# Three pairs of gate columns by Strassen, and the S5 branch in five steps per block

## The chip, the cores and the metric

The kernel runs on one core of a Trainium2 chip. The metric is the time of one execution on the device, in microseconds. The core has a matrix engine (TensorE, PE in the profile), whose weight loads are shown apart (PEld), three engines for elementwise work (VectorE or DVE, ScalarE or ACT, GpSimd or POOL) and a queue that issues transfers (SyncE or SP). Each engine executes its own instructions strictly in the order in which they were written, and waits at an instruction until what it reads has been written and what it overwrites has been read.

## The reference

One layer of a decoder trunk for 1024 tokens of width 1024, all in float32, cut to what matters here:

```
h = rms_norm(x, g_pre)
proj = h @ w_in
s5_x, s5_g, lru_x, lru_g, gate_s, gate_l = split(proj)   # 512, 512, 1280, 1280, 1024, 1024 columns
y_s = s5_ssm(s5_x, ...)                  # complex diagonal recurrence over the tokens
y_s = glu(gelu(y_s) @ w_glu) * silu(s5_g);  z_s = y_s @ w_bs
y_l = rg_lru(conv(lru_x), ...);             z_l = (y_l * silu(lru_g)) @ w_bl
merged = sigmoid(gate_s) * z_s + sigmoid(gate_l) * z_l
x = x + rms_norm(merged @ w_out, g_post)
x = x + (p @ w_ple) * sigmoid(x @ w_ple_gate)
```

The result must keep float32 accuracy. Each matrix product is therefore three products of rounded operands: high x high, high x low and low x high part.

## The kernel before, in words

Tensors lie transposed: 128 channels on the partitions, tokens along the row. h is four operands (B11, B21 for the first 512 tokens, input rows 0 to 511 and 512 to 1023; B12, B22 for the other 512), each in a high and a low part. `w_in` is 44 columns of 128 outputs. A column takes 8 row blocks x 2 token halves x 3 = 48 products of 128x512 (function `rows`), accumulated in PSUM, and `light` passes it through a sigmoid on ScalarE and stores it. Columns 36 to 43 are gate_l, 28 to 35 gate_s, 4 and 5 part of s5_g.

The class `Weights` streams weights: SP loads chunks of eight 128x128 blocks into four raw buffers; for every four blocks ("quad") ScalarE writes the high part into one of six ring buffers (L222) and VectorE the low part (L234), four quads ahead of TensorE. For some weights the low part is made by ScalarE and an accumulating transfer that GpSimd issues (L226).

The order is written by hand for TensorE, VectorE, ScalarE and GpSimd; only SP's order comes from the scheduler. Small work runs beside the columns: generators in the list `bg` are advanced one step by each `tick()`, and `rows` ticks after every 12 products, four times per column. A step only says where instructions stand in each engine's order; an engine may be ahead of TensorE or late.

S5 is such a generator. First the parameters (`prep`), on VectorE and then on GpSimd; three idle ticks; the ladders (`s5_ladders`: two tables of powers by doubling, 4 and 3 steps of four VectorE operations); "powers" (`powers_zoh`, seven VectorE operations, L669 to L675); `turn`: pwT, four transposes of it on TensorE (L691), evicted by ScalarE and sent through HBM (pt_d) into every block's wn. Then eight blocks (`s5_main`), a block seven ticks apart from the next:

1. VectorE multiplies wn (L913, L915);
2. the block before is finished: output products py (L983, L984), GELU on ScalarE; the next block's loads are issued;
3. products pkt on TensorE, four copies kt on ScalarE, an addition, and eight transfers that spread kt into the matrix toep, which py reads;
4. products pin (L939);
5. ScalarE copies pin to pq, VectorE rotates it by the tables (ta, tb, q); GpSimd makes the next block's output weights ca (L902 to L904, its middle operation waits for the toep transfers, since it writes the buffer of kt);
6. the scan (L960) and the rotation back; 7. the last four operations q (L971, L972), which py reads.

The next block's table (`s5_table`) is spread over these steps. After S5 its memory goes to the LRU branch. The later stages (`w_bl`, `w_out`) already use Strassen's scheme with seven half-size products.

## Time and profile before

| | |
|---|---|
| median of 3 runs | 928.81 us (928.27 to 928.93) |
| the profiled execution: time, span | 928.25 us, 926.5 us |
| gate columns and S5 (77.8 to 300.5 us) | 18 columns of 48 products and 8 blocks |
| DMA over the span | 134.21 MB, mean 145 GB/s |

A row of the timeline gives start, duration, engine, line, operation, output and inputs, shapes and count; in brackets how long the engine sat idle before it and what ended that. A row of a window gives, for each engine, busy time and number of instructions, then the granted clock, the busy share of the DMA engines and GB/s. A matmul's shown duration is longer than its distance to the next, since matmuls overlap; what a product costs is read from start to start. A 128x128 product on unrounded float32 counts as two instructions.

### The profile page before, as it was taken

The numbers are of one execution on the slowest core, as the hardware profiler recorded it, in microseconds if no ns is written. First come the engines' busy times: TensorE is split into PE (matmuls) and PEld (weight loads), VectorE is DVE, ScalarE is ACT, GpSimd is POOL, SyncE is SP. The second block draws the span as 40 slices with busy tenths as digits, with TensorE's granted clock in tenths as the row PEclk, the third lists the DMA queues.
The fourth block names the chain that finished last, engine by engine and source line by source line (L and its number), as shares of the span: only waits on it lengthen the run. The fifth ranks groups of instructions, "written<-read, shape, count | busy, mean of one in ns | idle before, by whom it ended". The sixth has DMA issues, their size and how long they took to land.

```text
span 926.5 us, 11716 instructions
## 1 busy us (share of the span) xinstructions
PE 919.0 (99%) x4228; PEld 760.3 (82%) x4228; DVE 624.6 (67%) x977; ACT 469.1 (51%) x714; POOL 150.6 (16%) x159
## 2 busy tenths in 40 slices
PE   9999999999999999999999999999999999999997
PEld 7888888888888888888888888888888887887886
DVE  6885566666664347766666767687862798886863
ACT  6643233444443356666666668544534355558531
POOL 1218112212220000000000000022322126422100
PEclk9999999999999999999999999999999999999999
DMA  9745445564533201111111116811479975499951
GB/s 358 277 126 160 126 142 166 172 171 133 173 97 113 74 29 52 52 46 51 52 52 52 47 34 216 291 56 55 141 255 244 247 193 206 119 245 233 301 184 56
DMA packets 70442, 134.21 MB, mean 145 GB/s; under 512 B 18416, under 2 KB 32880, under 8 KB 70384
## 3 DMA queue, kind: packets, MB, share of 16 engines
q1 hardware_dynamic: 64768, 122.72, 41.7%
q0 software_dynamic: 5472, 10.49, 6.3%
q8 instruction: 33, 0.54, 0.2%
q10 hardware_dynamic: 144, 0.26, 0.1%
q14 instruction: 25, 0.20, 0.1%
HBM read 95.30 MB, written 27.53 MB: 133 GB/s over the span
## 4 chain that ended last, share of the span: by engine, by line
PE 89%; issue 6%; DMA 2%; DVE 1%; POOL 1%; ACT 0%; POOLq 0%; SPq 0%
PE ps_L L319 16%; PE ps_L L317 8%; PE ps_rx L319 8%; PE ps_rg L319 8%; PE ps_rg L317 4%; PE ps_rx L317 4%; PE ps_F L319 3%; PE ps_u L319 3%; PE bZ L319 3%; PE ps_pg L319 2%; PE bW L319 2%; PE pg L319 2%; PE bX L319 2%; PE ps_ple L319 2%; PE ps_ea L319 2%
## 5 line engine op out<-in xcount | busy, mean ns | idle before, releaser
L319 PE MATMUL ps_L<-hB,wq 128*128 128x512 f32 x640 | 197.4, 390 | 0.0
L319 PEld LDWEIGHTS ps_L<-hB,wq 128*128 128x128 f32 x640 | 120.3, 188 | 24.3
L317 PE MATMUL ps_L<-hB,wq 128*128 128x512 f32 x320 | 127.1, 397 | 0.0
L222 ACT ACTIVATE wq<-wraw 128x512 fp32r<-128x512 f32 (+1 forms) x188 | 112.5, 613 | 24.1 <-issue 9.2
L234 DVE TENSOR_TENSOR wq<-wraw,wq 128x512 fp32r<-128x512 f32 (+1 forms) x152 | 105.0, 706 | 3.1 <-ACT wq L222 3.1
L319 PE MATMUL ps_rg<-hB,wq 128*128 128x512 f32 x320 | 98.5, 389 | 0.0
L319 PE MATMUL ps_rx<-hB,wq 128*128 128x512 f32 x320 | 98.5, 389 | 0.0
L319 PE MATMUL ps_pg<-x1hl,wq 128*128 128x512 f32 x240 | 74.9, 392 | 0.3 <-DVE x1hl L1374 0.2
L317 PEld LDWEIGHTS ps_L<-hB,wq 128*128 128x128 f32 x320 | 60.2, 188 | 13.3 <-issue 1.7
L319 PEld LDWEIGHTS ps_rg<-hB,wq 128*128 128x128 f32 x320 | 60.1, 188 | 12.5
L319 PEld LDWEIGHTS ps_rx<-hB,wq 128*128 128x128 f32 x320 | 60.1, 188 | 12.4
L194 POOL TENSOR_TENSOR wS<-wraw 128x512 f32<-128x512 f32 x8 | 12.4, 1549 | 354.8 <-DMA wraw<-w_blocks 343.3
L1078 DVE SCALAR_TENSOR_TENSOR c<-ps_rx,cp_t,c 128x1023 f32<-128x1023 f32 (+2 forms) x30 | 38.5, 1282 | 46.2 <-ACT c L1076 45.5
L317 PE MATMUL ps_rx<-hB,wq 128*128 128x512 f32 x160 | 62.3, 389 | 0.0
L317 PE MATMUL ps_rg<-hB,wq 128*128 128x512 f32 x160 | 62.3, 389 | 0.0
L319 PEld LDWEIGHTS ps_pg<-x1hl,wq 128*128 128x128 f32 x240 | 44.8, 188 | 11.5 <-DVE x1hl L1374 1.7
L1015 ACT ACTIVATE sg<-ps_L 128x1024 f32<-128x1024 f32 x20 | 20.5, 1027 | 59.7 <-issue 52.5
L226 POOL DMA_DIRECT2D wq<-wraw x36 | 31.8, 883 | 100.1 <-ACT wq L225 65.6
L317 PE MATMUL ps_pg<-x1hl,wq 128*128 128x512 f32 x120 | 47.0, 391 | 0.0
L319 PE MATMUL ps_u<-hB,wq 128*128 128x512 f32 x128 | 39.8, 392 | 0.4 <-DVE hB L736 0.4
L319 PE MATMUL ps_F<-ys,wq 128*128 128x512 f32 x128 | 39.4, 389 | 0.0
L1086 ACT ACT_TABLE_LOAD x9 | 11.5, 1283 | 51.2 <-DVE yr L1115 51.2
(360 smaller groups left out, 1927.0 us busy)
## 6 DMA issues: line engine op xcount, KB each, us to landing
wraw<-w_blocks SPq DMA_DIRECT2D x95, 512.0 KB
wq<-wraw POOLq DMA_DIRECT2D x36, 256.0 KB, 6.0
xt<-x_t SPq DMA_DIRECT2D x8, 512.0 KB
ple_d<-ple_sb SPq DMA_DIRECT2D x8, 512.0 KB
wn<-sbt SPq DMA_DIRECT2D x8, 512.0 KB
sgl_d<-sg SPq DMA_DIRECT2D x8, 512.0 KB
wn<-pt_d SPq DMA_DIRECT2D x16, 256.0 KB
sgs_d<-sg SPq DMA_DIRECT2D x8, 512.0 KB
```

Of the source, the lines that this page charges most:

```text
L194: G.tensor_tensor(s[name], s[a], s[b], op)
L222: nc.scalar.activation(hi, src, AF.Copy)
L226: nc.gpsimd.dma_start(lo.bitcast(F32), src, accum_op=ALU.add)
L234: self.nc.vector.tensor_tensor(lo, src, hi.bitcast(F32), ALU.subtract)
L317: T.matmul(ps, wh, xh, start=start, stop=False, skip_group_check=more)
L319: T.matmul(ps, a, b, start=False, stop=stop and a is (wh if xl_last else wl), skip_group_check=more)
L1015: S.activation(t, ps, AF.Sigmoid)
L1078: V.scalar_tensor_tensor(c[:, d:], ps[:, :NT - d], w_[3 - d], c[:, d:], ALU.mult, ALU.add)
L1086: S.activation(sq, ps, AF.Sigmoid)
```

## The change

Columns 30 to 35 of `w_in` are made in three pairs (30 and 31, 32 and 33, 34 and 35). With a pair's weights cut into A11, A12 (column m, input rows 0 to 511 and 512 to 1023) and A21, A22 (column m + 1), the pair is

```
S1 = A21 + A22   S2 = S1 - A11   S3 = A11 - A21   S4 = A12 - S2
T1 = B12 - B11   T2 = B22 - T1   T3 = T2 - B11    T4 = B21 - T2
u = A11*B11      z = u + S2*T2   w = S1*T1
column m:     first tokens u + A12*B21      other tokens z + w + S4*B22
column m + 1: first tokens z + S3*T3 + A22*T4      other tokens z + w + S3*T3
```

Seven products of four blocks (12 products of 128x512 each) stand for eight. The two of the first line's column m (bank lX) come first for all three pairs, then the other five pair by pair (banks lZ, two halves z and w). For these columns VectorE makes the sums S that GpSimd makes for `w_bl`, and the low parts of the plain quads and of A22 go the way by transfer.

The T need h in float32, so each of its eight row blocks is written to HBM (`h_d`) when it is made, and quarters of it come back into pages (`h_load`). T1 and T2 are subtracted on VectorE beside the last two S5 blocks (`t_early`), T3 and T4 after S5, where all four are also cut into high and low parts (`t_build`), with four pages and two buffers in the memory that S5 gave back.

S5's steps 1 and 2, and 3 and 4, are merged, so that a block takes five ticks. Columns 4 and 5 come first now, and S5 runs beside these two and the ten columns 36 to 43, 28 and 29. The ladders and the first table are a generator of their own (`s5_first`) ahead of `s5_all` in the list, the idle ticks are gone, and powers follow the end of `prep` by one tick and `turn` by two.

```
@@ -60,8 +61,16 @@
     plain(col("w_in", 2, lo) + col("w_in", 0, hi))
     plain(col("w_in", 1, hi) + col("w_in", 2, hi))
     plain(col("w_in", 3, range(ND)))
-    for m in (*range(36, 44), *range(28, 36), 4, 5):
+    for m in (4, 5, *range(36, 44), *range(28, PAIRS[0])):
         plain(col("w_in", m, range(ND)))
+    for m in PAIRS:
+        c = chunk(col("w_in", m, range(ND)))
+        light.add(c)
+        cut(c)
+    for m in PAIRS:
+        c0, c1 = (chunk(col("w_in", m + i, range(ND))) for i in range(2))
+        light.add(c0)
+        quads.extend((part, c0, c1, 4) for part in ("O2", "S1", "S3", "S4", "A22"))

     def gated(m, head):
         c = chunk(col("w_in", m, range(ND)))
...
@@ -191,7 +201,7 @@
                     s[name] = self.tmp.tile([P, HT], F32, tag=name, name=f"w{name}_{i}")
                 else:
                     s[name] = s[into]
-                G.tensor_tensor(s[name], s[a], s[b], op)
+                (self.nc.vector if light else G).tensor_tensor(s[name], s[a], s[b], op)

             if q[0] == "plain":
                 _, c, o, n = q
...
@@ -205,7 +215,7 @@
                 add("S1", "A21", "A22", ALU.add)
                 add("S2", "S1", "A11", ALU.subtract)
             if q[0] in ("S4", "O4"):
-                add("S4", "A12", "S2", ALU.subtract, "S2")
+                add("S4", "A12", "S2", ALU.subtract, "A12" if light else "S2")
             if q[0] == "S3":
                 add("S3", "A11", "A21", ALU.subtract, "A21")
             self.ready.append((s[q[0].replace("O", "S")], 4))
...
@@ -221,7 +231,8 @@
             lo = t[:, 1].rearrange("p b m -> p (b m)")[:, :n * P]
             nc.scalar.activation(hi, src, AF.Copy)
             q = QUADS[i]
-            if q[0] == "plain" and BLOCKS[q[1][0]][0] in self.BY_DMA and i < len(QUADS) - 2 * ND:
+            if q[0] in ("plain", "A22") and (q[1] in LIGHT or BLOCKS[q[1][0]][0] in self.BY_DMA
+                                             and i < len(QUADS) - 2 * ND):
                 nc.scalar.activation(lo, src, AF.Copy, scale=-1.0)
                 nc.gpsimd.dma_start(lo.bitcast(F32), src, accum_op=ALU.add)
             else:
...
@@ -734,6 +746,7 @@
         for h in range(2):
             hi, lo = hplain(k, h)
             (G if h and k else V).tensor_tensor(lo, xt(k, HALF[h]), hi.bitcast(F32), ALU.subtract)
+        nc.sync.dma_start(h_d[k], xt(k))

     def h_pages(names):
         for n, i0 in names:
...
@@ -917,9 +930,10 @@
         G.tensor_tensor(
             dd, ident[:16, :16].unsqueeze(1).to_broadcast([16, 4, 16]),
             d_skip[:, 4 * hb:4 * hb + 4].unsqueeze(2).to_broadcast([16, 4, 16]), ALU.mult)
-        yield
         before()
         s5_load(hb + 1)
+        if hb == 7:
+            h_load(2, "T2", "B22")
         yield

         kt = wk.tile([P, 576], F32, tag="kt", name=f"kt{hb}")[:16, :HT].rearrange("p (g m) -> p g m", g=4)
...
@@ -927,16 +941,16 @@
         for g in range(4):
             T.matmul(ps[32 * g:32 * g + 16, :P], bb_1[:, 4 * hb + g, :],
                      ca[:, g, 0:8, :].rearrange("p d c -> p (d c)"), start=True, stop=True, tile_position=(0, 32 * g))
+        pin = px.tile([P, 2, 2, P], F32, tag="px", name=f"pin{hb}")
+        for g in range(4):
+            T.matmul(pin[:, g // 2, g % 2, :], win[:, g, :], U[:, g, :], start=True, stop=True)
         for g in range(4):
             S.activation(kt[:, g, :], ps[32 * g:32 * g + 16, :P], AF.Copy)
         V.tensor_tensor(kt[:, :, 0:16], kt[:, :, 0:16], dd, ALU.add)
         for j in range(8):
             nc.sync.dma_start(toep[j::8, :, 16 * j:P], kt[:, :, 0:P - 16 * j])
-        yield
-
-        pin = px.tile([P, 2, 2, P], F32, tag="px", name=f"pin{hb}")
-        for g in range(4):
-            T.matmul(pin[:, g // 2, g % 2, :], win[:, g, :], U[:, g, :], start=True, stop=True)
+        if hb == 7:
+            h_load(6, "T4", "B21")
         next(table, None)
         yield

...
@@ -992,19 +1006,22 @@
     def s5_all():
         for _ in prep:
             yield
-        for _ in range(3):
-            yield
-        yield from s5_ladders()
+        yield
         turned[0]()
         yield
-        yield
         turn()
         yield
         s5_load(0)
-        yield from s5_table(0)
+        h_load(7, "T1", "B12")
+        yield
+        h_load(8, "T3", "B11")
+        yield
+        yield
         s5_out_weights(0)
         before = lambda: None
         for hb in range(8):
+            if hb == 6:
+                bg.append(t_early())
             before = yield from s5_main(hb, s5_table(hb + 1) if hb < 7 else iter(()), before)
         yield
         before()
...
@@ -1030,16 +1047,126 @@
             u_half(3, h, u3[:, HALF[h]], up[:, HALF[h]])
         yield

+    lf = {}
+
+    def t_subs(n, a, b):
+        for k in range(4):
+            V.tensor_tensor(lf[n][:, k], lf[a][:, k], lf[b][:, k], ALU.subtract)
+            if k % 2:
+                yield
+
+    def t_early():
+        yield from t_subs("T1", "T1", "T3")
+        while "T2" not in lf:
+            yield
+        yield
+        yield
+        yield from t_subs("T2", "T2", "T1")
+
+    def h_load(i, t, n):
+        lf[t] = quarter(page(i, f"f{t}", F32))
+        for k in range(4):
+            nc.sync.dma_start(lf[t][:, k], h_d[4 * (n[1] == "2") + k][:, HALF[n[2] == "2"]])
+
+    def s5_first():
+        yield from s5_ladders()
+        yield from s5_table(0)
+
     bg.append(u_last())
+    bg.append(s5_first())
     bg.append(s5_all())
+    for m in range(2):
+        light(4 + m, sil_d[m], True, ev_tile)
     for m in range(ND):
         light(36 + m, sgl_d[m], False, ev_tile)
-    for m in range(ND):
+    for m in range(PAIRS[0] - 28):
         light(28 + m, sgs_d[m], False, ev_tile)
-    for m in range(2):
-        light(4 + m, sil_d[m], True, ev_tile)
     drain()
     s5x.close()
+
+    gctx = ExitStack()
+    gp = gctx.enter_context(tc.tile_pool(name="gp", bufs=1))
+    page_pool.update({i: gp for i in (14, 15, 16, 17)})
+    lop = {"T2": [3, 14], "T1": [15, 16], "T3": [17, 2], "T4": [7, 8]}
+
+    def lpage(n, i):
+        lop[n][i] = quarter(page(lop[n][i], f"l{n}{i}"))
+
+    def t_low(n):
+        for k in range(4):
+            V.tensor_tensor(lop[n][1][:, k, :], lf[n][:, k], lop[n][0][:, k, :].bitcast(F32), ALU.subtract)
+
+    def t_high(n):
+        lpage(n, 0)
+        for k in range(4):
+            S.activation(lop[n][0][:, k, :], lf[n][:, k], AF.Copy)
+
+    def t_build():
+        t_high("T2")
+        lpage("T2", 1)
+        t_low("T2")
+        yield
+        t_high("T1")
+        lpage("T1", 1)
+        t_low("T1")
+        yield
+        yield from t_subs("T3", "T2", "T3")
+        t_high("T3")
+        yield from t_subs("T4", "T4", "T2")
+        lpage("T3", 1)
+        lpage("T4", 0)
+        for k in range(4):
+            S.activation(lop["T4"][0][:, k, :], lf["T4"][:, k], AF.Copy)
+        t_low("T3")
+        yield
+        lpage("T4", 1)
+        t_low("T4")
+
+    def lprod(ps, op, start):
+        W.ahead()
+        for k, wb in enumerate(W.next()):
+            three(ps, wb, (op[0][:, k, :], op[1][:, k, :]), start and k == 0, k == 3, not start)
+
+    def gate_out(m, h, t, src):
+        S.activation(t, src, AF.Sigmoid)
+        nc.sync.dma_start(sgs_d[m - 28][:, HALF[h]], t)
+
+    bg.append(t_build())
+    lu = quarter(page(9, "lu", F32))
+    for p_, m in enumerate(PAIRS):
+        x_ = wide(f"lX{p_}")[:, HALF[0]]
+        o = gp.tile([P, NT], F32, tag="c", name=f"lo{p_}", bufs=2)[:, HALF[0]]
+        lprod(x_, hq["B11"], True)
+        S.activation(lu[:, p_], x_, AF.Copy)
+        tick()
+        tick()
+        lprod(x_, hq["B21"], False)
+        gate_out(m, 0, o, x_)
+        tick()
+        tick()
+    for p_, m in enumerate(PAIRS):
+        z, w_ = (v[:, HALF[i]] for v in (wide(f"lZ{p_}"),) for i in range(2))
+        c = gp.tile([P, NT], F32, tag="c", name=f"lc{p_}", bufs=2)
+        gb, o = (c[:, HALF[i]] for i in range(2))
+        u = lu[:, p_]
+        lprod(z, lop["T2"], True)
+        V.tensor_tensor(z, z, u, ALU.add)
+        S.activation(u, z, AF.Copy)
+        tick()
+        lprod(w_, lop["T1"], True)
+        S.activation(gb, w_, AF.Copy)
+        V.tensor_tensor(w_, w_, u, ALU.add)
+        tick()
+        lprod(z, lop["T3"], False)
+        V.tensor_tensor(gb, gb, z, ALU.add)
+        gate_out(m + 1, 1, gb, gb)
+        tick()
+        lprod(w_, hq["B22"], False)
+        gate_out(m, 1, u, w_)
+        lprod(z, lop["T4"], False)
+        gate_out(m + 1, 0, o, z)
+    drain()
+    gctx.close()

     lctx = ExitStack()
     l1 = lctx.enter_context(tc.tile_pool(name="l1", bufs=1))
```

How instructions now stand. VectorE after the parameters, at the powers (pzt; etab is a ladder, wq_ a weight's low part). Before, both ladders stand ahead of them; the last rows of the second, then the powers:

```order
L853 TENSOR_TENSOR etab<-etab,cosp 128x32x4
L854 TENSOR_TENSOR etab<-etab,sinp 128x32x4
L855 TENSOR_TENSOR etab<-etab 128x16x4
L856 TENSOR_TENSOR etab<-etab 128x16x4
L669 TENSOR_TENSOR pzt<-pw,scratch 128x256
L670 TENSOR_TENSOR pzt<-pw,scratch 128x256
L671 TENSOR_TENSOR pzt<-pzt 128x256
```

and in the changed kernel, with the first ladder's last rows (128x16x8) ahead and the second ladder behind:

```order
L868 TENSOR_TENSOR etab<-etab 128x16x8
L869 TENSOR_TENSOR etab<-etab 128x16x8
L681 TENSOR_TENSOR pzt<-pw,scratch 128x256
L682 TENSOR_TENSOR pzt<-pw,scratch 128x256
L683 TENSOR_TENSOR pzt<-pzt 128x256
L684 TENSOR_TENSOR pzt<-pw,scratch 128x256
L685 TENSOR_TENSOR pzt<-pw,scratch 128x256
L686 TENSOR_TENSOR pzt<-pzt 128x256
L687 TENSOR_TENSOR pzt<-pzt,sgn 128x256
L245 TENSOR_TENSOR wq_830<-wraw_555,wq_830 128x512
L860 MEMSET etab 128x16
L861 MEMSET etab 128x16
```

The powers have moved ahead of the second ladder, and on TensorE pwT, which reads them, from behind 108 products of gate columns to behind 36.

ScalarE in an S5 block (kt and pq are the copies of pkt and pin; sg a gate's sigmoid, ysb S5's GELU), before:

```order
L931 ACTIVATE kt_2272<-pkt_2273 16x128 x4
L222 ACTIVATE wq_2312<-wraw_1936 128x512
L946 ACTIVATE pq_2327<-pin_2303 64x256 x4
L1015 ACTIVATE sg_2362<-ps_L_2254 128x1024
L222 ACTIVATE wq_2366<-wraw_2032 128x512
```

and now, in block 1:

```order
L1000 ACTIVATE ysb_1166<-py_1167 128x512
L1032 ACT_TABLE_LOAD
L1032 ACTIVATE sg_1187<-ps_L_1073 128x1024
L232 ACTIVATE wq_1191<-wraw_833 128x512
L948 ACTIVATE kt_1208<-pkt_1209 16x128 x4
L960 ACTIVATE pq_1248<-pin_1214 64x256 x4
```

The copies of pkt and of pin now follow each other, one tick behind the GELU of the block before.

ScalarE where the pairs begin, in the changed kernel (lu is the copy of an X product, lT a high part of a T, lo the sigmoid of the finished half column):

```order
L1000 ACTIVATE ysb_2299<-py_2300 128x512
L1032 ACT_TABLE_LOAD
L1032 ACTIVATE sg_2314<-ps_L_2229 128x1024
L232 ACTIVATE wq_2326<-wraw_1952 128x512
L236 ACTIVATE wq_2326<-wraw_1952 128x512
L1140 ACTIVATE lu<-lX_2324 128x512
L1102 ACTIVATE lT_2343<-fT_2148 128x512 x4
L1102 ACTIVATE lT_2353<-fT_948 128x512 x4
L232 ACTIVATE wq_2363<-wraw_1952 128x512
L236 ACTIVATE wq_2363<-wraw_1952 128x512
L1131 ACTIVATE lo_2325<-lX_2324 128x512
L232 ACTIVATE wq_2395<-wS_42_2373 128x512
```

At this place stood the copies and evictions of the first LRU column.

9 lines of the change are left out of this document (6 added, 3 removed).

## The prediction

> **What bounds the kernel now.** I read the page first, then TensorE's waits, then the timeline of the stretch the change rewrites (77 to 300 us), engine by engine. Part 1 of the page and the list of who waited, TensorE alone:
>
> ```profile
> PE 919.0 (99%) x4228; PEld 760.3 (82%) x4228; DVE 624.6 (67%) x977; ACT 469.1 (51%) x714; POOL 150.6 (16%) x159
> ...
> PE warm L500 <- DVE halfpi L291: 1.1, 1, 1.1
> PE ps_ple L317 <- DVE p_hi L526: 0.8, 1, 0.8
> PE ps_u L319 <- DVE hB L736: 0.4, 1, 0.4
> PE oY L319 <- DVE wq L234: 0.3, 1, 0.3
> PE ps_pg L319 <- DVE x1hl L1374: 0.2, 1, 0.2
> ```
>
> These are all of TensorE's waits, 2.8 us in sum, and the tile of the gate columns (ps_L) is not among them. So fewer products mean less time, one for one, and so does every new wait of TensorE mean more: no idle time is left that could take it up. The question is whether the other engines still hand TensorE everything in time when the order is packed tighter.
>
> **The products removed.** Three pairs of gate columns cost 96 products each; as seven half-products of 12 they cost 84. That is 36 fewer. One column of 48 runs from the first row here to the second:
>
> ```profile
> 300.55 0.39 PE L317 MATMUL ps_rx<-hB,wq 128*128 128x512 f32 x1
> 311.43 0.39 PE L317 MATMUL ps_rg<-hB,wq 128*128 128x512 f32 x1
> ```
>
> 10.88 us / 48 = 0.2267 us each, so 36 x 0.2267 = **-8.2 us**. The small products of S5 are the same number.
>
> **The transpose pwT, moved six ticks forward.** TensorE executes in order, and pwT needs the seven operations "powers" on VectorE. Before, 108 products of gate columns stood ahead of pwT; now 36. The gate columns start at 77.8, so TensorE reaches pwT at 77.8 + 36 x 0.2267 = 86.0. When can VectorE be done? Its rows, GpSimd's, both over 11 us, and pwT:
>
> ```profile
> L317 PEld LDWEIGHTS ps_L<-hB,wq x320: 186/188/193, 77.8 to 566.2; 128*128 128x128 f32 x160
> ...
> 81.10 1.99 DVE L234 TENSOR_TENSOR wq<-wraw,wq 128x512 fp32r<-128x512 f32 x3
> 84.36 0.20 DVE L855 TENSOR_TENSOR etab<-etab 128x32 f32<-128x32 f32 x1
> 84.47 1.06 DVE L856 TENSOR_TENSOR etab<-etab 128x32 f32<-128x32 f32 x1
> 93.86 1.55 DVE L856 TENSOR_TENSOR etab<-etab 128x128 f32<-128x128 f32 x1
> 98.24 0.42 DVE L669 TENSOR_TENSOR pzt<-pw,scratch 128x256 f32<-128x256 f32 x1
> 100.61 0.43 DVE L675 TENSOR_TENSOR pzt<-pzt,sgn 128x256 f32<-128x256 f32 x1
> ...
> 84.16 0.26 POOL L659 TENSOR_TENSOR scratch<-scratch,sgn 128x32 f32<-128x32 f32 x1
> 84.38 1.09 POOL L681 TENSOR_TENSOR bb<-braw,scratch 128x512 f32<-128x512 f32 x1
> 94.05 1.21 POOL L902 TENSOR_TENSOR ca<-pw,cc 128x576 f32<-128x576 f32 x1
> ...
> 84.30:95.30 11.00, 11.00 (x50) 9.10 (x50) 10.86 (x12) 2.06 (x3) 10.73 (x10) 1.00 0.59 183
> 102.49 0.60 PE L691 MATMUL pwT<-ident,pzt 128*128 128x128 f32 x4
> ```
>
> Between 84.3 and 95.3 GpSimd runs ten operations and VectorE only twelve: one VectorE operation passes per GpSimd operation, whatever its own length (84.36 takes 0.20, its like at 84.47 takes 1.06). GpSimd's work stands in the same order in the changed kernel and starts from the same point, so this crowding stays where it is. VectorE's order is now two weight corrections, the first ladder (16 operations), the seven powers. With one correction less ahead (1.99/3 = 0.66 us) and one less inside, about 14 of these remain at 84.3; some ten or eleven pass by 95.3, the last three or four at (101.04 - 98.24)/7 = 0.40 follow. VectorE ends at about 96.8, and TensorE waits 96.8 - 86.0 = **+10.8 us**. Bounds: had GpSimd been idle, the ladder's last two steps would take some 2.2 (steps of half the size take 0.4 to 0.7 uncrowded) and the powers 2.8 from 84.2, so +3.3; with the ladder ending as before (95.4), powers behind it and a start 2 late, +14.
>
> After such a gap TensorE may restart slowly. Its first rows show that state, and the last stretch the granted clock after idle time:
>
> ```profile
> 5.63 0.77 PE L317 MATMUL ps_ple<-p_hi,wq 128*128 128x512 f32 x1 [0.79 <-DVE p_hi L526]
> 9.59 0.63 PE L319 MATMUL ps_ple<-p_lo,wq 128*128 128x512 f32 x1
> 10.89 0.39 PE L317 MATMUL ps_ple<-p_hi,wq 128*128 128x512 f32 x1
> 920.00:927.00 7.00, 1.83 (x16) 1.63 (x14) 1.37 (x5) 0.45 (x2) 0.00 (x0) 0.87 0.11 37
> ```
>
> From 5.63 to 10.89 twelve products take 5.26 instead of 2.72 us: 2.5 lost, some of it waiting. Between nothing and 2.5 I take **+1.3**, the middle. The Trainium skill (TensorE: Matmul & The Clock Gate, What's actually happening) says that an idle window of 3.4 us halves the clock and a busy one frees it; by that rule the restart costs an estimated 3.4/2 = 1.7 and the sum would be 0.4 higher. No gap here before the tail is long enough to show it.
>
> **S5 in five ticks.** Before, pin and the output product py of a block stand 60 products apart, now 48; the recurrence between them must be done by then. Four of the eight blocks, pin and last q:
>
> ```profile
> 122.56 1.05 PE L939 MATMUL pin<-U,wn 128*128 128x128 f32 x8
> 135.11 0.42 DVE L972 TENSOR_TENSOR q<-ta,tb 64x254 f32<-64x254 f32 x1
> 211.84 1.05 PE L939 MATMUL pin<-U,wn 128*128 128x128 f32 x8
> 225.80 0.42 DVE L972 TENSOR_TENSOR q<-ta,tb 64x254 f32<-64x254 f32 x1
> 256.49 1.05 PE L939 MATMUL pin<-U,wn 128*128 128x128 f32 x8
> 268.51 0.42 DVE L972 TENSOR_TENSOR q<-ta,tb 64x254 f32<-64x254 f32 x1
> 278.81 1.05 PE L939 MATMUL pin<-U,wn 128*128 128x128 f32 x8
> 288.29 0.42 DVE L972 TENSOR_TENSOR q<-ta,tb 64x254 f32<-64x254 f32 x1
> 293.31 0.38 PE L983 MATMUL py<-U,toep 128*128 128x128 f32 x2
> ```
>
> pin to py took 293.31 - 278.81 = 14.5 us; now 14.5 - 12 x 0.2267 = 11.8. The recurrences took 13.0, 14.4, 12.4 and 9.9 (the last block has no GpSimd work and no tables beside it); all eight ended inside 14.5, seven end outside 11.8. In order they exceed it by 1.2, 0.9, 0.6, 0.9, 2.6, 0.6 and 0.6: **+7.3 us**. Block 7 keeps 60. Lower bound 0, if GpSimd's share, which now starts later after pin, falls behind the last q (the 9.9 is such a case). Upper bound 14: ScalarE now does the four copies of kt (1.1 us) between pin and the reads of pin, in blocks 1 and 5 the gate's sigmoid stands ahead of them, and block 6 gets T's subtractions; about 1 more per block.
>
> **The pairs.** Each X product is evicted by ScalarE and at once continued in the same bank, so TensorE waits for the eviction three times, with nothing between. What ScalarE has queued when the first X product ends shows after a py:
>
> ```profile
> 183.27 0.39 PE L984 MATMUL py<-q,ca 128*128 128x128 f32 x2
> 183.73 1.28 ACT L986 ACT_TABLE_LOAD   x1 [7.86 <-issue]
> 185.02 0.60 ACT L986 ACTIVATE ysb<-py 128x512 f32<-128x512 f32 x1
> 187.98 1.28 ACT L1015 ACT_TABLE_LOAD   x1
> 189.28 1.02 ACT L1015 ACTIVATE sg<-ps_L 128x1024 f32<-128x1024 f32 x1
> ...
> 90.01 1.14 ACT L222 ACTIVATE wq<-wraw 128x512 fp32r<-128x512 f32 x2
> ```
>
> The last py now stands right before X: table, GELU, table, sigmoid, two weight copies and the eviction are 1.28 + 0.60 + 1.28 + 1.02 + 1.14 + 0.6 = 5.9 us, against 12 x 0.2267 = 2.7 of products: +3.2. Before the second eviction stand eight copies for T2 and T1, four more and the eviction, 13 x 0.55 = 7.2 against 5.4: +1.8. Before the third stand T3's and T4's copies, which wait for subtractions on VectorE: between 1.0, if copies and subtractions pass hand in hand, and 4, if VectorE's 19 operations of 0.66 run to their end first: +2.0. Sum **+7.0**; at least 3 x 1.0 (0.4 to the product's end, 0.6 eviction), at most 11 with a wait of 1 at some of the pairs' other hand-overs, for which 2.7 us of products stand against 2.0 of additions and copies, so I give them nothing.
>
> **At nothing.** The eight writes of h hold back three weight loads on SP, from 36.6 to about 49; TensorE uses the first at 67. VectorE takes over GpSimd's sums: 11 operations of 0.66 per pair beside 13.6 us of products. If that cover is gone, each late weight costs what it is late.
>
> Sum on the profiled execution (span 926.5, time 928.25; the median of the runs is 928.81): 928.25 - 8.2 + 10.8 + 1.3 + 7.3 + 7.0 = **946.5 us**.
>
> **Rivals.** (1) Slower, but the recurrence keeps up, because GpSimd's part slides behind it, and the X waits stay near 4: 928.25 - 8.2 + 10.8 + 1.3 + 0 + 4 = 936. For it: block 7's 9.9. Against: 12.4 and more in all others. (2) Every block late by a microsecond more and the X stage at its bound: 928.25 - 8.2 + 10.8 + 1.3 + 14 + 11 = 957. For it: ScalarE's new order. Against: a wait of TensorE lets the others catch up. (3) Faster: VectorE passes the ladder at its uncrowded pace, pwT waits 3.3 with no slow restart, S5 keeps up and the X waits are bare evictions: 928.25 - 8.2 + 3.3 + 3 = 926.4; it decides only if pwT can start by 89.3, and the row of twelve operations in 11 us speaks against it. (4) No change: as (3) with 2 us of the recurrence, 928.4.
>
> **How the numbers follow.** Forecast 0.52, rival 1 0.26, rival 2 0.14, rival 3 0.06, rival 4 0.02. The range 934 to 957 takes in the forecast and rival 1 and the near side of rival 2. A measurement of this kernel tells about 0.2% from no change: faster 0.06, same 0.02, slower 0.92.
>
> **What would show it.** Right: TensorE waits some 11 us for VectorE at pwT, its longest wait; then a few tenths to 2.6 us at py in blocks 0 to 6, for q; then three waits for ScalarE in the same bank at X. Products of 0.63 after the pwT wait show the slow restart. Wrong: no wait of TensorE at pwT (VectorE's powers done by 87), or waits for weights or DMA that I gave nothing; or S5's waits at pin instead of py (VectorE late with wn).

## The result: 41 us slower

The changed kernel takes 969.59 us (median of 4 runs, 968.36 to 972.46), the kernel before 928.54 (928.04 to 928.93) on the same chip: a ratio of 1.0447 (95% interval 1.0423 to 1.047). Forecast were 946.5 and a range of 934 to 957. The direction was right, the size was not: +41 instead of +18. The profiled execution took 968.36, its span is 966.4.

Part 1 of the page after (busy us, share of the span, instructions):

```profile
PE 922.8 (95%) x4192; PEld 755.8 (78%) x4192; DVE 661.7 (68%) x1030; ACT 493.3 (51%) x763; POOL 159.1 (16%) x168
```

And TensorE's longest waits in the list of who waited (the waiting operation and the one waited for; us in all, times, longest):

```profile
PE pwT L703 <- DVE pzt L683: 9.2, 1, 9.2
PE lX L329 <- ACT lu L1140: 6.2, 3, 3.1
PE py L998 <- DVE q L986: 5.2, 7, 2.2
PE lZ L329 <- DVE lZ L1158: 4.3, 3, 1.5
PE lZ L329 <- ACT lu L1154: 4.3, 3, 1.4
PE lZ L329 <- DVE lc L1161: 2.3, 3, 0.8
PE lZ L329 <- ACT lu L1131: 2.2, 3, 0.7
```

TensorE issues 36 products fewer and is nevertheless busy 3.8 us longer, so beside the waits some products ran slowly. The first three rows are the three places of the prediction, with waits somewhat under those it gave them. The four rows of lZ, 13.1 us, are a place to which it gave nothing.

By stretches of the changed kernel (gate columns to the first pkt; S5; the pairs), each row with the length, then TensorE's busy time and instructions, and behind POOL's the granted clock:

```profile
77.80:113.02 35.22, 25.12 (x102) 19.82 (x100) 25.10 (x54) 6.39 (x8) 15.41 (x27) 0.85 0.61 175
113.02:255.99 142.97, 137.24 (x738) 112.59 (x737) 114.03 (x210) 65.62 (x119) 40.07 (x31) 1.00 0.61 168
255.99:339.99 84.00, 64.67 (x256) 48.41 (x255) 38.48 (x61) 37.73 (x66) 4.26 (x5) 0.96 0.42 125
```

With 0.2267 us per product these rows give the terms. The first stretch holds 96 products (21.8) and pwT (0.35): 35.2 - 22.1 = 13.1 lost, forecast 10.8 + 1.3 = 12.1. In S5 the groups of py, pin and pkt take 31.6 us start to start instead of 22.8: 8.8 lost, forecast 7.3. The pairs hold 252 products, 57.1 us: **26.9 lost, forecast 7.0**. Sum: -8.2 + 13.1 + 8.8 + 26.9 = +40.6, measured on the profiled executions 968.36 - 928.25 = +40.1. Only the pairs were far off; of their 26.9, 10.2 lie in the X part (72 products from 256.0 to 282.5) and 16.7 in Z.

### The profile page after: what moved, and what is told of

Read it like the earlier page. It is cut to its first block, busy times and chain, and to the rows that moved or that the text cites. A ratio compares the mean times of both kernels' runs of the same rounds, so it can differ in the third digit from the quotient of the medians.

```text
span 966.4 us, 11838 instructions
## 1 busy us (share of the span) xinstructions
PE 922.8 (95%) x4192; PEld 755.8 (78%) x4192; DVE 661.7 (68%) x1030; ACT 493.3 (51%) x763; POOL 159.1 (16%) x168
## 4 chain that ended last, share of the span: by engine, by line
PE 65%; issue 3%; DMA 1%; DVE 1%; ACT 1%; POOL 0%; POOLq 0%; ACTq 0%
PE ps_rx L331 8%; PE ps_rg L331 8%; PE ps_pg L331 6%; PE ps_rg L329 4%; PE ps_rx L329 4%; PE ps_F L331 3%; PE ps_pg L329 3%; PE lZ L331 3%; PE bZ L331 3%; PE pg L331 2%; PE bW L331 2%; PE bX L331 2%; PE lZ L329 2%; PE ps_F L329 2%; PE ps_ea L331 1%
## 5 line engine op out<-in xcount | busy, mean ns | idle before, releaser
L331 PE MATMUL ps_L<-hB,wq 128*128 128x512 f32 x448 | 139.3, 392 | 0.0
L232 ACT ACTIVATE wq<-wraw 128x512 fp32r<-128x512 f32 (+1 forms) x191 | 114.7, 613 | 28.7 <-DMA wraw<-w_blocks 10.2
L245 DVE TENSOR_TENSOR wq<-wraw,wq 128x512 fp32r<-128x512 f32 (+1 forms) x146 | 101.7, 712 | 18.9 <-ACT wq L232 18.9
L331 PEld LDWEIGHTS ps_L<-hB,wq 128*128 128x128 f32 x448 | 85.0, 190 | 17.5
L329 PE MATMUL ps_L<-hB,wq 128*128 128x512 f32 x224 | 89.5, 399 | 0.0
L331 PEld LDWEIGHTS ps_rx<-hB,wq 128*128 128x128 f32 x320 | 60.1, 188 | 12.4
L237 POOL DMA_DIRECT2D wq<-wraw x45 | 39.5, 879 | 179.4 <-ACT wq L236 146.4
L204 POOL TENSOR_TENSOR wS<-wraw 128x512 f32<-128x512 f32 x8 | 12.2, 1520 | 339.8 <-DMA wraw<-w_blocks 328.2
L329 PEld LDWEIGHTS ps_L<-hB,wq 128*128 128x128 f32 x224 | 42.7, 191 | 8.4
L329 PEld LDWEIGHTS ps_rx<-hB,wq 128*128 128x128 f32 x160 | 30.0, 188 | 6.3
## 6 DMA issues: line engine op xcount, KB each, us to landing
wq<-wraw POOLq DMA_DIRECT2D x45, 256.0 KB, 5.7
fT<-h_d SPq DMA_DIRECT2D x16, 256.0 KB
wn<-pt_d SPq DMA_DIRECT2D x16, 256.0 KB
```

Of the source, the lines that this page charges most:

```text
L204: (self.nc.vector if light else G).tensor_tensor(s[name], s[a], s[b], op)
L232: nc.scalar.activation(hi, src, AF.Copy)
L237: nc.gpsimd.dma_start(lo.bitcast(F32), src, accum_op=ALU.add)
L245: self.nc.vector.tensor_tensor(lo, src, hi.bitcast(F32), ALU.subtract)
L329: T.matmul(ps, wh, xh, start=start, stop=False, skip_group_check=more)
L331: T.matmul(ps, a, b, start=False, stop=stop and a is (wh if xl_last else wl), skip_group_check=more)
```

## Experiments on the pairs

**Z: two tiles instead of one.** At a hand-over inside Z, TensorE's last products into one half, the first into the other, and what ScalarE and VectorE do between, in the changed kernel:

```profile
284.75 0.61 PE L331 MATMUL lZ<-lT,wq 128*128 128x512 f32 x2
286.79 0.50 PE L329 MATMUL lZ<-lT,wq 128*128 128x512 f32 x1 [1.42 <-ACT lu L1154]
...
285.40 0.70 DVE L1153 TENSOR_TENSOR lZ<-lZ,lu 128x512 f32<-128x512 f32 x1 [0.59 <-PE lZ L331]
...
286.14 0.60 ACT L1154 ACTIVATE lu<-lZ 128x512 f32<-128x512 f32 x1 [1.76 <-DVE lZ L1153]
```

The product at 286.79 (T1) writes w_, the second half of lZ. The addition and the copy read and write z, the first half. Its operands were there, and the bank that it writes was free; it starts when the copy of the other bank ends (286.14 + 0.60). Four such hand-overs per pair cost, start to start, 1.59, 1.64, 0.95 and 0.91 us more than a product: 5.09, in three pairs 15.3.

```
-        z, w_ = (v[:, HALF[i]] for v in (wide(f"lZ{p_}"),) for i in range(2))
+        z = px.tile([P, HT], F32, tag="px", name=f"lY{p_}")
+        w_ = wide(f"lZ{p_}")[:, HALF[1]]
```

> Edit: in the Z part of the pairs the two results z and w_ no longer lie in the two banks of one tile (lZ); z has a one-bank tile of its own, w_ stays in half of a wide one. Nothing else. In the changed kernel TensorE stands four times per pair at the hand-over from one half to the other (start to start 1.59, 1.64, 0.95 and 0.91 us more than a product takes, 5.09 per pair, 15.3 in all). Theory: these waits are for the tile and not for the data; the bank that TensorE wants to write is free. With two tiles they go, and the time falls by about 15 us, from 969.6 to about 954. Rival A, that TensorE waits for data of the same bank and the additions and copies are simply too slow for 12 products (2.7 us): the waits stay under other names, at most 4 us are gained, about 966. Rival B, that copies and additions slow down when products run beside them: half of it, about 962.

Measured: 952.66 us (ratio 1.0263, 1.0248 to 1.0279), 17 less than the changed kernel. The same place (z is now lY):

```profile
287.22 0.62 PE L331 MATMUL lY<-lT,wq 128*128 128x512 f32 x2
287.68 0.39 PE L329 MATMUL lZ<-lT,wq 128*128 128x512 f32 x1
...
287.88 0.70 DVE L1154 TENSOR_TENSOR lY<-lY,lu 128x512 f32<-128x512 f32 x1 [0.63 <-PE lY L331]
...
288.61 0.60 ACT L1155 ACTIVATE lu<-lY 128x512 f32<-128x512 f32 x1 [1.77 <-DVE lY L1154]
```

TensorE goes on 0.46 us after the start of two products, as anywhere, and addition and copy take as long as before beside it. All of Z's waits are gone: Z's 180 products take 40.8 us, which is 180 x 0.2267. The waits belonged to the tile, not to the data and not to the bank; both rivals fall.

**X: the B11 products first.**

```
-    for p_, m in enumerate(PAIRS):
-        x_ = wide(f"lX{p_}")[:, HALF[0]]
-        o = gp.tile([P, NT], F32, tag="c", name=f"lo{p_}", bufs=2)[:, HALF[0]]
+    xs_ = [wide(f"lX{p_}")[:, HALF[0]] for p_ in range(3)]
+    for p_, x_ in enumerate(xs_):
         lprod(x_, hq["B11"], True)
         S.activation(lu[:, p_], x_, AF.Copy)
-        tick()
-        tick()
+    tick()
+    tick()
+    for p_, m in enumerate(PAIRS):
+        x_ = xs_[p_]
+        o = gp.tile([P, NT], F32, tag="c", name=f"lo{p_}", bufs=2)[:, HALF[0]]
         lprod(x_, hq["B21"], False)
```

> Edit: the three B11 products of the pairs come first, in their three banks, each copied to lu, then the three B21 products that continue in these banks; the weights come in that order. Two other products (5.4 us) now stand between an eviction and the product that continues in its bank. The X part lost 10.4 us against its products in the changed kernel: waits of 3.1, 2.0 and 1.0 with what lies around them, and slow products behind the first two. Theory: waits and slow products go, the rest of the order keeps up; the time falls by 8 to 10, to about 960. Rival: ScalarE's and VectorE's chain of T1 to T4 sets the time of this part, so that what TensorE gains at X it waits at the first Z products; at most 3 gained, about 967.

Measured: 970.79 us (1.0462, 1.0445 to 1.048), no gain. The waits at X are gone, and one of the same size stands at the first hand-over of Z, as the list of TensorE's waits has it:

```profile
PE lZ L328 <- ACT lu L1155: 13.5, 3, 10.7
```

VectorE's timeline there (start, length, operation):

```profile
278.88 5.08 DVE L1096 TENSOR_TENSOR lT<-fT,lT 128x512 fp32r<-128x512 f32 x8
...
285.81 0.69 DVE L1154 TENSOR_TENSOR lZ<-lZ,lu 128x512 f32<-128x512 f32 x1
```

TensorE reached Z 8.9 us earlier (273.6 instead of 282.5), but the addition stands on VectorE behind sixteen operations for low parts, eight subtractions and the weights, and comes when these are through, at 285.8 (in the changed kernel 285.4). The rival held: at X the waits were cover for VectorE's queue.

**X first, two tiles, and the T's earlier.**

```
         yield from t_subs("T2", "T2", "T1")
+        t_high("T2")
+        lpage("T2", 1)
+        t_low("T2")
+        yield
+        while "T4" not in lf:
+            yield
+        yield from t_subs("T3", "T2", "T3")
+        yield from t_subs("T4", "T4", "T2")
```

> Edit, on top of the two tiles for z and w_ (952.7 us): the three B11 products come first, as in the run that had this alone (970.8: no wait at X, but 10.7 us at the first Z hand-over); and what VectorE and ScalarE build for T1 to T4 starts earlier: the subtractions for T3 and T4 stand behind those for T2 in the last S5 block, and T2's high and low part are made there too (T2's low part takes page 9, lu moves to page 14). In the run with X first alone, VectorE ran from 266.8 to 286.4 without a pause: 16 operations for low parts, 8 subtractions, the weights, and only then the addition that TensorE waited for. Theory: that queue is what set the time; 8 subtractions and 4 low parts (7.5 us) now lie in VectorE's pause at 252 to 259, the queue ends near 279 instead of 286, and with two tiles TensorE has 2.7 us more of products before it needs the sum; X and Z lose about 1 to 3 us in all instead of 10.3, time about 944. Rival: the chain of copies on ScalarE (8.6 us from 263 on, plus evictions and weights) still sets the time; the first Z products wait for T1 or T3, 5 us lost, about 948.

Measured: 945.87 us (1.0188, 1.0174 to 1.0202), 6.8 less than with the two tiles alone. The pairs now lose 2.8 us: 1.2 at the first Z hand-over, 0.6 for a weight, the rest in small pieces. That agrees with the reading that VectorE's queue, which ended at 286.4, had set the time: 7.5 us of it now lie in VectorE's pause. How much of the gain belongs to the order of X and how much to the earlier T's, no run separates.

## Experiments on pwT

**Ladders early.** The powers wait behind the ladder, and both are slowed by GpSimd; this takes the ladder away.

```
         yield "den"
+        s5_ladders()
         V.reciprocal(den, den)
...
     def s5_first():
-        yield from s5_ladders()
+        yield
+        yield
+        yield
         yield from s5_table(0)
```

> Edit: both ladders of the table are put ahead of the reciprocal on VectorE, into the 8.7 us in which VectorE waits for GpSimd; table 0 stays where it was. The seven powers now have no ladder ahead, GpSimd's bb and ca run beside them as before. In the changed kernel TensorE waits 9.2 + 0.9 us at pwT and some products behind it run slowly (about 12 us in all). Theory, one VectorE operation passes per GpSimd operation while GpSimd works: seven powers from 83.8 beside seven GpSimd operations of 1.1, 1.1, 1.4, 1.0, 1.2, 1.4 and 1.5 (8.7 us) end at about 92.5; pwT still waits some 6.5 us, the time falls by 3 to 4, to about 966. Rival, the ladder ahead was the whole cause and GpSimd does not hold powers up: they end at 83.8 + 7 x 0.40 = 86.7, the wait is under 1 us and the slow products go too, about 958.

Measured: 963.26 us (1.038, 1.0365 to 1.0396), 6.3 less. Powers on VectorE beside bb on GpSimd:

```profile
84.64 0.42 DVE L684 TENSOR_TENSOR pzt<-pzt 128x256 f32<-128x256 f32 x1
84.98 1.28 DVE L685 TENSOR_TENSOR pzt<-pw,scratch 128x256 f32<-128x256 f32 x1
86.19 1.27 DVE L686 TENSOR_TENSOR pzt<-pw,scratch 128x256 f32<-128x256 f32 x1
...
84.67 1.32 POOL L694 TENSOR_TENSOR bb<-braw,scratch 128x512 f32<-128x512 f32 x1
85.95 1.23 POOL L695 TENSOR_TENSOR braw<-braw,scratch 128x512 f32<-128x512 f32 x1
```

From the moment bb starts, each power lasts as long as the GpSimd operation beside it. Three powers had run before bb did, so the last ended at 90.0 and not at 92.5; pwT waited 3.9, not 6.5. The theory's pace is right, the starting point was not; the rival (end at 86.7) falls.

**GpSimd held.** A GpSimd operation that reads pzt is put ahead of bb, and bb behind the powers.

```
+        def bb_ops():
+            G.tensor_tensor(held, pzt[:, 512:544], sgn.to_broadcast([P, 32]), ALU.mult)
+            G.tensor_tensor(bb_1, b1, zrb, ALU.mult)
...
         turned[0]()
+        turned[2]()
```

> Edit: as with the ladders put early, and in addition GpSimd's three bb operations, and with them cc and ca behind, are held until the powers are done: one small GpSimd operation that reads pzt (128x32) stands ahead of them, and they are issued after the powers. With the ladders early alone, the powers L685 to L688 took 1.14 to 1.37 us each beside GpSimd's bb (1.2 to 1.3 each) instead of 0.42, pwT waited 3.9 us, some products behind it ran slowly, and the time was 963.3. Theory (one VectorE operation passes per GpSimd operation): the four powers take 0.42 again and end near 87, TensorE waits about 1 us at pwT and no products run slowly behind it; about 958. Rival A, the powers are slow by themselves (their broadcast operands): nothing changes, 963. Rival B: what GpSimd does later now comes late, pkt waits for ca, or the table and wn on VectorE are crowded instead and pin waits for wn; 961 to 965.

Measured: 962.60 us (1.0372, 1.0356 to 1.0388), no different from the ladders alone. It tested nothing: the columns 512 to 543 of pzt are written by the second power, and the operation went at 84.7, with the other powers still to come. With the last power's columns instead (256 to 287):

> Edit: ladders early and GpSimd held, as before, but the small GpSimd operation ahead of bb now reads the columns that the last power writes (256 to 287 of pzt) and not 512 to 543. In the earlier run that operation began at about 84.7, behind the second power, because its columns were written by then; GpSimd's bb ran beside the last powers again (1.16 to 1.37 us each), pwT waited 3.1 us, and the time (962.6) was that of the ladders alone (963.3). So holding was not tested there. Theory (one VectorE operation passes per GpSimd operation): now all seven powers take 0.42, the last ends near 86.8, TensorE, which arrives at 86, waits about 1 us and no products run slowly; about 958.5. Rival A, the powers are slow by themselves or by their place: nothing changes, 963. Rival B: the waits move to pkt (ca late) or pin (wn late): 961 to 965.

Measured: 960.98 us (1.0358, 1.0341 to 1.0374), and in its timeline the last power:

```profile
86.36 0.43 DVE L688 TENSOR_TENSOR pzt<-pzt,sgn 128x256 f32<-128x256 f32 x1
```

and in its list of waits TensorE's at pwT and at the first pin:

```profile
PE pin L950 <- issue: 3.5, 1, 3.5
...
PE pwT L731 <- DVE pzt L688: 0.6, 1, 0.6
```

Alone, every power takes 0.42 and pwT waits 0.6. But the first pin now waits 3.5, where no pin waited more than 0.5 with the ladders early alone: rival B, and the time gained at pwT was mostly spent there. The next section but one takes that wait away.

## Experiments on S5

**py later.** The block's output comes two ticks later, with the writes of toep and the load of U behind it.

```
-        before()
         s5_load(hb + 1)
...
-        for j in range(8):
-            nc.sync.dma_start(toep[j::8, :, 16 * j:P], kt[:, :, 0:P - 16 * j])
...
+        before()
+        for j in range(8):
+            nc.sync.dma_start(toep[j::8, :, 16 * j:P], kt[:, :, 0:P - 16 * j])
+        s5_load_u(hb + 1)
```

> Edit: in S5 the output product py of a block (with its GELU and the copies that start from it) comes two ticks later, one tick behind the next block's pin, so that 72 products instead of 48 stand between pin and py; the writes of toep and the load of U move behind it. Still five ticks per block. In the changed kernel TensorE waits 5.2 us at py (seven waits, the longest 2.2), and S5's py groups take 7.5 us more than in the kernel before. Theory: the recurrence takes 10 to 14 us and fits into 16; the waits at py go and nothing takes their place, the time falls by about 7, to about 962. Rival: the recurrence is a loop, and VectorE's work of a block is longer than five ticks, so that the wait moves to pin (VectorE late with wn) or to U; gain under 3, about 968.

Measured: 980.77 us (1.0564, 1.0548 to 1.058), 11 worse. No wait for q is left, but there is one of 1.8 us at a pin for wn, which VectorE makes, and there are six at pkt, each for GpSimd's last operation for ca, in the list of waits:

```profile
PE pkt L946 <- POOL ca L922: 11.3, 6, 2.5
```

and in GpSimd's timeline what the operation before that one waited for:

```profile
204.78 1.22 POOL L921 TENSOR_TENSOR t<-pw,cc 128x576 f32<-128x576 f32 x1 [9.14 <-DMA toep<-kt]
```

GpSimd's second operation (t) shares its memory with kt, and so waits for the eight writes of toep that read kt. With these later, ca is later. Behind four of the six waits some products ran slowly as well, so the run loses more than the waits alone. In the changed kernel the same wait for toep puts GpSimd beside the end of the recurrence; POOL, VectorE and TensorE there:

```profile
192.55 3.25 POOL L916 TENSOR_TENSOR t<-pw,cc 128x576 f32<-128x576 f32 x1 [10.21 <-DVE q L974]
195.88 1.46 POOL L917 TENSOR_TENSOR ca<-ca,t 128x576 f32<-128x576 f32 x1
...
194.65 1.43 DVE L985 TENSOR_TENSOR q<-ta,tb 64x254 f32<-64x254 f32 x1
196.09 1.52 DVE L986 TENSOR_TENSOR q<-ta,tb 64x254 f32<-64x254 f32 x1
...
197.67 0.49 PE L998 MATMUL py<-q,ca 128*128 128x128 f32 x2 [2.17 <-DVE q L986]
```

In this block the list names the scan (L974) as what ended GpSimd's wait of 10.21 us; t does not read q, and the last wait for toep before it had ended at 192.2. In the other six blocks the list names toep itself, 87.3 us in all.

**ca right behind py.** t takes pq's memory instead, and the three operations are issued behind the py of the block before.

```
-        t9 = wk.tile([P, 576], F32, tag="kt", ...)
+        t9 = wk.tile([P, 576], F32, tag="pq", ...)
...
         s5_load(hb + 1)
+        if hb < 7:
+            s5_out_weights(hb + 1)
...
-        if hb < 7:
-            s5_out_weights(hb + 1)
```

> Edit in S5 only: GpSimd's temporary t for the output weights ca shares its memory with pq instead of kt, and the three operations are issued right behind py of the block before. In the changed kernel the second of them (L916) waits for the eight writes of toep, which read kt and which SP issues over 5.4 us, and so runs at the end of the recurrence: there the first q operations (L985, L986) take 1.3 to 1.5 us each instead of 0.42. Theory: GpSimd's part now runs in the pause between py and pq, all q operations take 0.42, the recurrence ends about 2 us earlier, the waits of TensorE at py (5.2 us in seven) go to under 1; time down by 6 to 8, about 962.5. Rival A: GpSimd now crowds wn's two operations (L926, L928), and pin waits for them instead; down by at most 2, 968. Rival B: the recurrence is late for ScalarE's copies ahead of it (kt, then pq), not for GpSimd; the waits stay, 969.

Measured: 962.83 us (1.0369, 1.0353 to 1.0385), 6.8 less. The timeline at the same block, GpSimd and VectorE:

```profile
183.75 1.40 POOL L917 TENSOR_TENSOR ca<-ca,t 128x576 f32<-128x576 f32 x1
198.83 1.49 POOL L915 TENSOR_TENSOR ca<-pw,cc 128x576 f32<-128x576 f32 x1 [11.67 <-PE py L998]
...
195.59 0.40 DVE L985 TENSOR_TENSOR q<-ta,tb 64x254 f32<-64x254 f32 x1
196.00 0.42 DVE L986 TENSOR_TENSOR q<-ta,tb 64x254 f32<-64x254 f32 x1
```

and in its list of waits:

```profile
PE py L998 <- DVE q L986: 0.3, 2, 0.2
```

The waits at py fall from 5.2 to 0.3 us, and S5's groups from 31.6 to 25.2. Part of this is lost again: ca of block 1 now runs right behind that of block 0, from 93.3 on, and pwT waits 12.2 instead of 9.2. In the profiled executions the time falls by only 4.1, from 968.36 to 964.27. Neither rival held.

## All together, and a version faster than both

> All four edits together: two tiles for z and w_ and the pairs' new order with the T's early, ladders early with GpSimd held, ca right behind py. Theory: the losses lie in separate stretches and TensorE is the bound in all of them, so the gains add: 969.6 - 17 (two tiles, measured) - 8.5 (X) - 11.5 (pwT) - 7 (S5) = about 925.6, a little under the kernel before (928.2). Rival: a gain of one stretch is lost in the next, because the earlier TensorE arrives, the earlier it needs what others make (wn for the first pin, the weights' loads, T's); 930 to 935.

Two tiles, the pairs' new order, ladders early with the hold that did not hold, and ca behind py: 928.99 us (1.0007, 0.9998 to 1.0016), the same as the kernel before. Together the edits take back 40.6 of the 41 us. One by one they had gained 16.9 (two tiles), 6.8 (the pairs' order on top of them), 7.0 (ladders and hold) and 6.8 (ca), 37.5 in all; the 3 us that ca alone added at pwT are not there with the ladders early. The time is 3.4 above what was expected, of which 3.1 are pwT's wait that the hold did not remove. Two further steps, the true hold and T4's four low-part operations behind Z's first addition:

> All four edits together, as in the run that gave 929.0, with GpSimd held to the end of the powers. Theory: the 3.1 us at pwT and about 1.6 of slow products behind it shrink to about 1; 925. Rival: what GpSimd does later comes late (ca for pkt, and VectorE's table and wn behind it for pin): no gain, 929.

> The run before, and T4's four operations for its low part on VectorE stand behind the first addition of Z instead of ahead of it. In the run with all edits that gave 929.0, TensorE waited 0.5 us for a weight correction and 1.2 us for the copy of the first sum, for which VectorE was 2.5 us late with T4's low part ahead; in all X and Z lost about 2.9. Theory: 1.5 to 2 less than the run before, about 923. Rival: T4's low part is now late for its own product; 926 or more.

Measured: 930.84 (1.0029, 1.0017 to 1.004) and 929.91 (1.0017, 1.0008 to 1.0027), neither of them under 928.99. The rival held for the first: at pwT 0.6 instead of 3.1, but 4.1 at the first pin. SP's queue in the run that gave 930.84, and the GpSimd operation that holds braw's page:

```profile
90.07 1.69 SPq L1095 DMA_DIRECT2D fT<-h_d  x2
91.85 0.39 SPq L733 DMA_DIRECT2D pt_d<-pzt  x1
...
88.80 1.24 POOL L698 TENSOR_TENSOR braw<-braw,scratch 128x512 f32<-128x512 f32 x1
```

The transposed powers could have gone at about 88. In SP's order a read of h for T1 stands ahead of them, into the page that bb still reads; bb had been moved 2.5 us later by the hold. VectorE's table and weights ahead of wn were late as well: in the run that gave 929.91 they ended at 101.95, and wn's first operation waited 1.05 us more for its transfer. T4's later low part gained 0.9, about half of what was expected, and single runs of the two kernels overlap.

The last run ties these reads to blocks 1 and 2, and puts table 0 behind wn on VectorE:

```
+        if hb in (1, 2):
+            h_load(*((7, "T1", "B12"), (8, "T3", "B11"))[hb - 1])
...
         lf[t] = quarter(page(i, f"f{t}", F32))
+        if t in ("T1", "T3"):
+            V.memset(lf[t][:, :, 0:1], 0.0)
...
     def s5_first():
...
+        for _ in range(7):
+            yield
+        for _ in s5_table(0):
+            pass
```

> Edit, on top of the run that gave 929.9 (all edits, T4's low part late): the reads of h for T1 and T3 are tied to S5's blocks 1 and 2 (a small VectorE operation writes their first columns there) instead of standing on SP ahead of pt_d, and table 0 stands behind wn's two operations on VectorE instead of ahead of them. In that run TensorE waited 3.7 us at the first pin and then ran products slowly (about 1.7 us more): in its sister run the copy of pwT was long done when SP issued pt_d at 91.85, because a read of h ahead of it waited for the page that bb held until 90.0; and VectorE's table and weight work, crowded by GpSimd, ran to 102.0 ahead of wn's operations. Theory: pt_d is issued near 88.5, wn arrives by about 98, VectorE ends it near 100.5 where TensorE comes at 100.9; pin waits under 0.5 us; time 929.9 - 3.7 - 1.4 = about 925, under the kernel before (928.3). Rival A: the loads of wn themselves (some 6 us behind pt_d, beside the weights' loads) set it; half is gained, 927.5. Rival B: the reads of h now meet S5's own loads and toep's writes on SP, and a later block waits: no gain, 930.

Measured: 925.12 us against 928.25 (ratio 0.9968, 0.9956 to 0.998); all six times, up to 925.66, lie under all ten of the kernel before, from 927.79 on. Part 1 of its page:

```profile
PE 912.5 (99%) x4192; PEld 751.8 (81%) x4192; DVE 648.2 (70%) x1032; ACT 493.1 (53%) x763; POOL 162.2 (18%) x169
```

TensorE's three longest waits, none of them in the stretches that the change rewrites (0.5 us at py and 0.5 at pwT follow):

```profile
PE ps_ple L328 <- ACT wq L231: 1.1, 2, 0.6
PE warm L511 <- DVE halfpi L302: 1.1, 1, 1.1
PE ps_pg L330 <- DVE x1hl L1515: 0.5, 1, 0.5
```

and in SP's timeline the write of the transposed powers, 3.9 us earlier than in the run that gave 930.84:

```profile
87.97 0.37 SPq L733 DMA_DIRECT2D pt_d<-pzt  x1
```

TensorE is busy 99% again, with 36 products fewer: 912.5 us against 919.0. No run has one of the two last steps alone; by the times above, the reads moved alone would have left VectorE's queue, and the table moved alone the late transfer. This is the change with most of its waits taken out, 0.3% faster than the kernel before and 4.6% faster than the change as it was made.

## Why the prediction was wrong

**The products** (-8.2): borne out as far as the runs go. In the last run TensorE is busy 919.0 - 912.5 = 6.5 us less, while S5's groups of py, pin and pkt still take 25.7 us start to start instead of 22.8 and the pairs 1.8 more than their 252 products.

**pwT** (+10.8, +1.3): right in mechanism and about in size (13.1). The waits are 9.2 + 0.9 = 10.1; the other 3.0 are slow products behind them, more than twice the 1.3 and over the 2.5 given as its most. The changed kernel's first and last power, and the second pair of transposes:

```profile
94.22 0.41 DVE L681 TENSOR_TENSOR pzt<-pw,scratch 128x256 f32<-128x256 f32 x1
96.59 0.42 DVE L687 TENSOR_TENSOR pzt<-pzt,sgn 128x256 f32<-128x256 f32 x1
...
97.07 0.69 PE L703 MATMUL pwT<-ident,pzt 128*128 128x128 f32 x2 [0.90 <-DVE pzt L687]
```

VectorE ended at 97.0 (forecast 96.8), and that it came so close is luck: GpSimd was through at 94.15 and not at 95.3, and by then only nine ladder operations had passed beside it where ten or eleven were counted, so that all seven powers, and not three or four, followed at 0.40 each. That one VectorE operation passes per GpSimd operation was read off one stretch of the trace; the powers with and without GpSimd beside them (1.3 and 0.42 us) show it. The Trainium skill (SBUF — State Buffer, SBUF: two separate sides) says that the two engines share a port pair that one of them holds for a whole instruction, also where VectorE reads two operands from SBUF; these rows agree with it.

**S5** (+7.3): right in place and about in size (8.8: the waits for q at py are 5.2 of it). The excesses forecast from the old distances held in the worst block, 2.3 us against 2.6, but not block by block: the seven waits lie in blocks 0, 4, 5 and 6 (1.1, 2.3, 1.1 and 0.7 us), and blocks 1 to 3, which were given 0.9, 0.6 and 0.9, have none. Rival 1's condition, that GpSimd's part slides behind the last q, came half: it slides, but only as far as the writes of toep let it, and that is the end of the recurrence, where it stretches the last q operations. The prediction's sum left that link through the shared memory out.

**The X products** (+7.0): the first two waits came as counted, 3.1 and 2.0 (forecast 3.2 and 1.8); the third was 1.0, its lower bound, and not 2.0. The term was 10.2, since behind the first two waits products ran at about half speed (some 3.0 us lost), for which the prediction had a term at pwT alone.

**The Z products** (nothing): the step that failed. "2.7 us of products stand against 2.0 of additions and copies, so I give them nothing" takes it that TensorE may write one half while the other is evicted. Both halves are one tile, and the program waits for the whole of it: additions and copies, instead of lying beside 2.7 us of products, lie between them. The times of the additions were sized well enough; they were put beside the path instead of on it, four times in each of three pairs, 15.3 us. The upper bound of the term did allow a wait of 1 at some of these hand-overs; it came at all twelve, with 0.9 to 1.6. The forecast with this term at its measured value is 946.5 + 15.3 = 961.8; with the 3.2 more at X and the 2.5 more at pwT and S5 it is 967.5, against 968.36.

**The rivals**: none of the four was this one. All of them moved the sizes of the terms already listed, while the missing one was a wait at a place where the count of instructions looked balanced.

## What to carry to other kernels

Before calling an eviction "covered by products into the other half", look whether the halves are one tile: here the list of waits names ScalarE's copy of z as what the product into w_ waited for. Two accumulators that take turns belong in two tiles. A wait of the bound engine may be the cover of another engine's queue: taking it away (X first) is worth nothing until that queue is shorter too; so measure the waits one by one, but judge the version with all of them gone. And an operand buffer shared by two helpers (t and kt) ties an engine's timing to a transfer of the other one.

## What the runs showed of the hardware

Short waits can cost twice. Behind a wait of 3.14 us and one of 2.00 us products ran at 0.427 us each instead of 0.2267 for some 3 us (changed kernel, the X part):

```profile
262.11 0.79 PE L329 MATMUL lX<-hB,wq 128*128 128x512 f32 x1 [3.14 <-ACT lu L1140]
262.70 1.05 PE L331 MATMUL lX<-hB,wq 128*128 128x512 f32 x2
263.55 0.63 PE L329 MATMUL lX<-hB,wq 128*128 128x512 f32 x1
...
271.25 0.50 PE L329 MATMUL lX<-hB,wq 128*128 128x512 f32 x1 [2.00 <-ACT lu L1140]
271.59 0.76 PE L331 MATMUL lX<-hB,wq 128*128 128x512 f32 x2
272.14 0.63 PE L329 MATMUL lX<-hB,wq 128*128 128x512 f32 x1
272.57 1.05 PE L331 MATMUL lX<-hB,wq 128*128 128x512 f32 x2
```

About 1.3 and 1.7 us are lost so, on top of the waits. Behind the second wait they begin only 0.9 us after TensorE has restarted. The waits of 1.4 to 1.5 us in Z, two in each pair, were followed by no slow product. The wait of 2.17 us at py had no slow products behind it in the changed kernel (at 199 us) but had them, from the same 2.17, in the run with the pairs reordered: whether a wait of this length costs twice varies from run to run. Nor does the length alone decide: with GpSimd held by the second power's columns a wait of 3.09 us at pwT had no slow product behind it, and with the last power's columns one of 3.50 us at the first pin had none, while one of 1.26 us at py (236 us) had them in the run with the pairs reordered. The Trainium skill (TensorE: Matmul & The Clock Gate, What's actually happening) names an idle window of about 3.4 us, free-running, after which the clock is halved. The half speed about agrees (0.427 against 0.2267), and so does the free-running window with the varying start; but here waits of 2.0 us were enough, where by the idle window as stated they should have cost nothing. What share of such a window has to be idle, no run here settles.
